# Two of the late modulation pairs are made in the second mixer's heads instead of the first FFN, with a smaller scratch for dynamic transfers

## The chip, the cores and the metric

The kernel runs on one core of one Trainium2 chip. The metric is device time in microseconds of one execution. Before the change the median of three runs is 1742.76 us (1740.17 to 1743.3).

## What is computed

Two layers of a diffusion backbone over 512 latent tokens and 256 context tokens of width 1024. Each layer has a mixer and a SwiGLU FFN (hidden width 2816), each between norms with a shift, scale and gate. The mixer of the first layer is gated linear attention beside grouped-query attention; that of the second is a bidirectional gated recurrence (HGRN2) with eight heads of 128. Only the latent tokens are returned.

The part that moves is the modulation. Each layer turns two vectors, one for latent tokens (`c`) and one for context tokens (`c_ctx`), into six vectors of 1024:

```python
sc = jax.nn.silu(c)
scc = jax.nn.silu(c_ctx)
for l in range(DEPTH):
    m_lat = jnp.split((sc @ mod_w[l] + mod_b[l])[:, None, :], 6, axis=-1)
    m_ctx = jnp.split((scc @ mod_w[l] + mod_b[l])[None, None, :], 6, axis=-1)
    h_lat = _modulate(_rms(x_lat, norm_pre_mix[l]), m_lat[0], m_lat[1])
    ...
    x_lat = x_lat + m_lat[2] * _rms(o_lat @ w_out, norm_post_mix[l])
    h_lat = _modulate(_rms(x_lat, norm_pre_ffn[l]), m_lat[3], m_lat[4])
    x_lat = x_lat + m_lat[5] * _rms(_swiglu(h_lat, ffn_w_gate[l], ffn_w_up[l], ffn_w_down[l]), norm_post_ffn[l])
```

In the last layer the context tokens end after the mixer's scan, so of its vectors 2, 3, 4 and 5 only the latent versions are needed. Vector 2 is first used behind the second mixer's heads, in its output projection; 3, 4 and 5 later still.

## The kernel before

Products of full precision are made of three products of rounded parts (`mm3`, L679): a weight is loaded raw, ScalarE rounds it to a high part and VectorE subtracts that for the low part (`unit`, L664 to L674). Such weight units go round in three raw buffers and four buffers of parts. SP issues all weight loads, in one queue.

The order: first mixer, output projection, first FFN (`ffn`, L1488), second mixer (`odd_mixer`, L1298), output projection, second FFN. A scheduler orders the instructions of each engine. Where `self.pinned` is set, TensorE's products stay in the order in which the program issues them; this holds for the heads of the second mixer and not for the FFN. The other engines' orders are the scheduler's in both.

**Modulation vectors** that are not needed at once are made on VectorE (`mod_vec`, L508 to L551), a generator that takes one small step whenever it is asked. For each job (two vectors) it loads `mod_w` in blocks of 128 x 1024 (512 KB, L454, two buffers `mraw`), one block ahead, and multiplies each block by a column of the activated vector into an accumulator (`macc`, L528 for the first block, L530 for the others). A job that makes latent and context versions of one vector has 8 blocks of two passes; a job with two vectors for the latent tokens alone has 16 blocks of one pass. Then TensorE sums the accumulators over the partitions (L537), VectorE copies the sum (`modrows`, L462), TensorE turns it (`modT`, L468) and VectorE adds the bias (L474). Where the vector is a gate, it is multiplied by a norm's gain (L576), turned (`gcT`, L580), copied (L582) and stored to DRAM (L584), from where it is later read as a row for all partitions. `modrows` and the gate's copy take turns in the same two `mraw` buffers.

**The first FFN** runs a loop over pairs of hidden blocks. A round has two products of gate and up weights by a seven-product scheme (`seven`, L768), whose weight sums VectorE makes (`pair_operands`, L730), and a product with the down weights for six token tiles, added to `y` on VectorE (L820). `fill` asks the modulation generator for a step at two places in `seven` and at the end of each token tile. All five jobs of `late_mods` (L1755) stand there.

**The second mixer.** First come value products (`odd_values`), then a loop over eight heads (L1415). A head has three weight units: two forget gates (`ff`, with a sigmoid on ScalarE at L1320) and the query (`fq`). Its recurrence (`scan`, L858) multiplies keys and queries by decays in seven doubling levels: at each level ScalarE copies half of the array (L923) and VectorE multiplies it (L928) and the decays (L929). TensorE makes small products from the levels (`pch`, `pbh`), turns the array (`knph`), makes the states' increments (`pdh`), and VectorE chains the states (L995); then TensorE makes the output (`poh`), and VectorE and GpSimd norm it (L1388, L598, L600, L1390). The loop interleaves three generators: `new` is the next head's products, `scan` and `outs` the recurrences of the heads before; `go` asks each of those named for one step.

Of the kernel before, what the change touches and what calls it, by code (L numbers as in the profile page):

```python
# [30 lines left out]
R_C, R_CC, R_NPM, R_MB, R_NQM, R_NPF, R_NQF, R_BG, R_LB, R_GG, R_HG, R_END = 0, 8, 16, 32, 128, 144, 160, 176, 180, 212, 213, 214  # L31
# [285 lines left out]
class Net:  # L317
# [980 lines left out]
    def odd_mixer(self, h, fi):  # L1298
        nc, I = self.nc, self.I
# [4 lines left out]
        with self.pool("hg") as gp:  # L1304
# [73 lines left out]
            def head(hd, arr, q, ks, f, S0):  # L1378
                def V(t, hh):
                    return fi[:, t, hd * P : (hd + 1) * P]  # L1380

                def evac(hh, t0, n, po):
                    o = fi[:, 0:LT, hd * P : (hd + 1) * P]
                    nc.scalar.copy(o, po)
                    sq = gp.tile([P, LT, P], F32, tag="sq", bufs=1, name="sq")
                    nc.scalar.activation(sq, po, AF.Square)
                    ss = self.sm.tile([P, LT], F32, tag="ss4", name="ss4")
                    nc.vector.tensor_reduce(ss, sq, axis=AX.X, op=ALU.add)  # L1388
                    rs = self.rstd(ss, P, LT)
                    nc.vector.tensor_tensor(o, o, rs[:, :, None].to_broadcast([P, LT, P]), op=ALU.mult)  # L1390

                return self.scan(gp, f"h{hd}", arr, q, ks, 1.0, f, LT, 1, V, S0, None, evac)

            def gate(c0):
                us = self.nat_units(w, 4 * D + c0, 256, 0) + self.nat_units(w, 4 * D + c0, 256, 1)

                def eo(t0, pt):
                    s = self.wp.tile([P, WU], F32, tag="mraw", bufs=2, name="silu")[:, :512].rearrange("p (a n) -> p a n", a=2)
                    nc.scalar.activation(s, pt[:, :, :256], AF.Silu)
                    o = fi[:, t0 : t0 + 2, c0 : c0 + 256]  # L1400
                    nc.vector.tensor_tensor(o, o, s, op=ALU.mult)

                for t0 in (0, 2):
                    self.gemm_nat(w, 4 * D + c0, 256, h, (t0,), eo, us=us)
                    yield
# [3 lines left out]
            def go(*xs):  # L1409
                for x in xs:  # L1410
                    next(x, None)

            self.pinned = True
            outs = old = scan = iter(())
            for hd in range(8):  # L1415
                given = []
                new = prep(hd, given)
                go(scan, new)
                go(outs, old)
                go(new, new)  # L1420
                go(outs, old, scan)
                go(new, new)
                go(scan, scan)
                outs, old, scan = scan, new, head(hd, *given[0])
            g = [gate(c0) for c0 in (0, 256, 512, 768)]
            go(scan, g[0])
            go(outs, old)
# [161 lines left out]
    def run(self):  # L1589
        nc, I, out = self.nc, self.I, self.out  # L1590
# [164 lines left out]
        def late_mods(pool):  # L1755
            return self.mod_vec(
                pool,
                (
                    (0, ((5, 0), (5, 1)), (5, R_NQF)),
                    (1, ((0, 0), (0, 1)), None),  # L1760
                    (1, ((1, 0), (1, 1)), None),
                    (1, ((2, 0), (3, 0)), (2, R_NQM, 1)),
                    (1, ((4, 0), (5, 0)), (5, R_NQF, 1)),
                ),
            )

        def ending(ys):
# [19 lines left out]
            return ender(ep, 0, 5, order, xat(x1), only_lat(xat(x2)), (1, 1, 0, R_NPM), h1), values(), ep  # L1787

        ys = self.ffn(0, ha, yp, fp, pp, rp, forms, ending, late_mods)
        fp.release()  # L1790

# [73 lines left out]
```

## Time and profile before

| What | Value |
|---|---|
| Median of three runs | 1742.76 us |
| Span of the profiled execution | 1746.0 us |
| The profiled execution's own time | not given apart from its span |
| Instructions | 33377 |
| DMA | 187.26 MB, mean 107 GB/s |
| ScalarE busy | 864.0 us (49%) |
| GpSimd busy | 73.5 us (4%) |

A profile is of one execution. Its lines give the source line, the engine (PE is TensorE, PEld its weight loads, DVE is VectorE, ACT is ScalarE, POOL is GpSimd, SP issues transfers), the operation, what is written from what, its shape, and how often. Matmuls are pipelined, so two of them overlap in the records and their spacing from start to start says what one costs. A wait is given as who waited for whom, with the total, the number of times and the longest.

### The profile page before, as it was taken

The page shows a single profiled execution, that of the slowest core. Times are in us where ns is not written, and L with a number is a line of the kernel's source. Part 1 is how long each engine was busy: PE and PEld are TensorE (multiplying, and loading weights), DVE is VectorE, ACT ScalarE, POOL GpSimd, SP SyncE. Part 2 cuts the span into 40 slices and gives each one's busy share as a digit, 9 for nine tenths or more (in the row PEclk, how much of TensorE's full clock was granted, in tenths as well). Part 3 has the DMA queues.
Part 4 walks back from the last instruction along what each step waited for, and adds up shares of the span by engine and source line. Part 5 has one row for each costly group of instructions (what it writes and reads, how often), then busy time and mean ns, then how long its engine had stood idle before and what let it go on. Part 6 is the DMA issues. An engine that isn't in the chain of part 4 may idle for free. (4 is left out here: it accounts for less than half of the span.)

```text
span 1746.0 us, 33377 instructions
## 1 busy us (share of the span) xinstructions
PE 1692.6 (97%) x13992; PEld 1536.0 (88%) x13992; DVE 1288.6 (74%) x2062; ACT 864.0 (49%) x1502; POOL 73.5 (4%) x93
## 2 busy tenths in 40 slices
PE   7999999999999999999999999999999999999998
PEld 5899987888999889898998998889898899999997
DVE  4889668736969999796668228887864678878785
ACT  4745567746442323333347336666643754344342
POOL 1004110000000000000001000000000000000000
PEclk9999999999999999999999999999999999999999
DMA  9641022144335465452234222111114333233333
GB/s 318 196 139 39 2 72 88 52 139 136 118 88 155 133 187 174 131 163 71 61 105 161 85 73 62 48 52 50 60 52 133 121 100 106 86 107 101 97 106 121
DMA packets 173937, 187.26 MB, mean 107 GB/s; under 512 B 6454, under 2 KB 149340, under 8 KB 173788
## 3 DMA queue, kind: packets, MB, share of 16 engines
q1 hardware_dynamic: 171856, 181.56, 33.6%
q10 hardware_dynamic: 1932, 3.59, 0.6%
q8 instruction: 109, 1.79, 0.4%
q14 instruction: 40, 0.33, 0.1%
HBM read 175.66 MB, written 9.46 MB: 106 GB/s over the span
## 5 line engine op out<-in xcount | busy, mean ns | idle before, releaser
L673 DVE TENSOR_TENSOR wL<-raw,wH 128x1024 fp32r<-128x1024 f32 (+1 forms) x126 | 151.0, 1205 | 114.7 <-ACT wH L672 114.5
L348 PE MATMUL nat<-wH,x 128*128 128x256 f32 (+1 forms) x1216 | 229.1, 287 | 3.0 <-ACT x L641 2.6
L727 ACT CAST wH<-raw 128x1024 fp32r<-128x1024 f32 x120 | 124.6, 1052 | 178.5 <-PE acc L348 70.8
L348 PEld LDWEIGHTS nat<-wH,x 128*128 128x128 f32 x1216 | 191.9, 191 | 8.0 <-ACT x L641 3.6
L728 DVE TENSOR_TENSOR wL<-raw,wH 128x1024 fp32r<-128x1024 f32 x120 | 145.1, 1219 | 64.0 <-ACT wH L727 64.0
L672 ACT CAST wH<-raw 128x1024 fp32r<-128x1024 f32 (+1 forms) x126 | 129.0, 1039 | 104.0 <-PE nat L348 31.4
L348 PE MATMUL acc<-wH,gH 128*128 128x512 f32 x440 | 172.6, 393 | 0.0
L348 PE MATMUL nat<-wL,x 128*128 128x256 f32 (+1 forms) x608 | 172.6, 284 | 0.0
L348 PE MATMUL acc<-wH,gL 128*128 128x512 f32 x440 | 171.7, 390 | 0.0
L348 PE MATMUL acc<-wL,gH 128*128 128x512 f32 x440 | 171.6, 390 | 0.0
L820 DVE TENSOR_TENSOR y<-y,acc 128x1024 f32<-128x1024 f32 x135 | 114.7, 861 | 31.6 <-PE acc L348 28.3
L348 PE MATMUL ff<-x,wH 128*128 128x512 f32 (+1 forms) x512 | 127.6, 340 | 0.0
L530 DVE SCALAR_TENSOR_TENSOR macc<-mraw,scT,macc 128x1024 f32<-128x1024 f32 x98 | 122.7, 1276 | 5.7 <-DMA mraw<-in_mod_w_dram 5.3
L600 POOL TENSOR_TENSOR rs<-ms,neghalf 128x1 f32<-128x1 f32 (+2 forms) x62 | 57.5, 928 | 1598.0 <-DVE ms L598 1597.9
L348 PEld LDWEIGHTS nat<-wL,x 128*128 128x128 f32 x608 | 116.5, 192 | 0.0
L348 PE MATMUL oproj<-wH,x 128*128 128x512 f32 x320 | 102.9, 398 | 3.6 <-ACT x L1235 3.6
L348 PEld LDWEIGHTS acc<-wH,gH 128*128 128x128 f32 x440 | 82.6, 188 | 19.8 <-issue 1.7
L348 PEld LDWEIGHTS acc<-wH,gL 128*128 128x128 f32 x440 | 82.6, 188 | 17.4
L348 PEld LDWEIGHTS acc<-wL,gH 128*128 128x128 f32 x440 | 82.7, 188 | 16.0
L348 PEld LDWEIGHTS ff<-x,wH 128*128 128x128 f32 x512 | 87.2, 190 | 10.1 <-issue 0.2
L923 ACT COPY qkh<-arr 128x512 f32<-128x512 f32 x112 | 70.1, 642 | 36.2 <-DVE arr L928 32.1
L348 PE MATMUL ff<-x,wL 128*128 128x256 f32 (+1 forms) x256 | 86.2, 337 | 0.0
(344 smaller groups left out, 4068.4 us busy)
## 6 DMA issues: line engine op xcount, KB each, us to landing
mraw<-in_mod_w_dram SPq DMA_DIRECT2D x80, 512.0 KB, 3.9
raw<-in_ffn_w_gate_dram SPq DMA_DIRECT2D x44, 512.0 KB, 3.8
raw<-in_ffn_w_up_dram SPq DMA_DIRECT2D x44, 512.0 KB, 4.5
raw<-in_ffn_w_down_dram SPq DMA_DIRECT2D x44, 512.0 KB, 3.6
raw<-in_odd_w_in_dram SPq DMA_DIRECT2D x40, 512.0 KB, 3.8
mraw<-in_mod_w_dram SPq DMA_DIRECT2D x32, 256.0 KB, 6.0
raw<-in_even_w_in_dram SPq DMA_DIRECT2D x16, 512.0 KB, 4.0
x<-xr SPq DMA_DIRECT2D x14, 512.0 KB, 2.7
```

Of the source, the lines that this page charges most:

```text
L348: return self.pin(self.nc.tensor.matmul(*a, **k))
L530: nc.vector.scalar_tensor_tensor(a, u, w, a, op0=ALU.mult, op1=ALU.add)
L600: nc.gpsimd.tensor_tensor(rs, ms, self.neghalf.to_broadcast([P, w]), op=ALU.pow)
L672: nc.scalar.copy(H[:, :m], raw[:, :m])
L673: nc.vector.tensor_tensor(L[:, :m], raw[:, :m], H[:, :m].bitcast(F32), op=ALU.subtract)
L727: self.nc.scalar.copy(H, f)
L728: self.nc.vector.tensor_tensor(L, f, H.bitcast(F32), op=ALU.subtract)
L820: nc.vector.tensor_tensor(y, y, pt, op=ALU.add)
L923: nc.scalar.copy(qkv[:, :, :, half, :], dst)
```

## The change

The last two jobs leave the FFN's list. The second mixer makes a generator of its own for them, with its accumulators in the heads' pool, and each of the six calls of `go` in a head's turn also asks it for a step; what is left after the eight heads is run out there. The program's scratch for dynamic transfers is set to 512 bytes per partition; before, it had its default size.

```diff
+            mods = self.mod_vec(gp, ((1, ((2, 0), (3, 0)), (2, R_NQM, 1)), (1, ((4, 0), (5, 0)), (5, R_NQF, 1))))
             self.pinned = True
             outs = old = scan = iter(())
             for hd in range(8):
                 given = []
                 new = prep(hd, given)
-                go(scan, new)
-                go(outs, old)
-                go(new, new)
-                go(outs, old, scan)
-                go(new, new)
-                go(scan, scan)
+                go(scan, new, mods)
+                go(outs, old, mods)
+                go(new, mods, new)
+                go(outs, old, scan, mods)
+                go(new, new, mods)
+                go(scan, scan, mods)
                 outs, old, scan = scan, new, head(hd, *given[0])
+            for _ in mods:
+                pass
...
                     (1, ((1, 0), (1, 1)), None),
-                    (1, ((2, 0), (3, 0)), (2, R_NQM, 1)),
-                    (1, ((4, 0), (5, 0)), (5, R_NQF, 1)),
...
-    nc = bacc.Bacc("TRN2", target_bir_lowering=False, num_devices=1)
+    nc = bacc.Bacc("TRN2", target_bir_lowering=False, num_devices=1, dynamic_dma_scratch_size=512)
```

Line numbers of the changed kernel are higher by one to three behind L1412.

## The prediction

> **What bounds the kernel now.** I read the page's first part, the stretches of time (windows) of the two stages that the change touches, then the timelines and waits inside them.
>
> ```profile
> PE 1692.6 (97%) x13992; PEld 1536.0 (88%) x13992; DVE 1288.6 (74%) x2062; ACT 864.0 (49%) x1502; POOL 73.5 (4%) x93
> ```
>
> TensorE is busy for 97% of a span of 1746.0 us, so almost any removed or added TensorE work counts in full, and VectorE's work counts only where TensorE must wait for it. The windows' columns are the stretch, its length, and busy time with counts of PE, PEld, DVE, ACT and POOL, then the granted clock.
>
> ```profile
> 616.10:807.50 191.40, 188.39 (x993) 170.98 (x992) 165.70 (x206) 65.51 (x91) 0.00 (x0) 1.00 0.51 156
> 840.16:886.54 46.38, 46.06 (x242) 42.56 (x242) 30.78 (x40) 16.15 (x22) 0.00 (x0) 1.00 0.23 68
> 977.00:1036.00 59.00, 59.00 (x470) 57.84 (x469) 8.74 (x9) 14.37 (x18) 0.00 (x0) 1.00 0.19 54
> 1089.86:1121.37 31.51, 31.51 (x400) 28.04 (x399) 25.12 (x56) 19.69 (x34) 1.44 (x1) 1.00 0.18 52
> ```
>
> The first row is four rounds of the first FFN's loop over hidden blocks, with the two moved pairs in them; VectorE is busy for 165.70 of 191.40 us and TensorE idles 3.0 us. The second is one round of the same loop after the modulation has ended: 46.38 us. The third lies between the FFN and the first head's recurrence: TensorE is full, VectorE has 50 us of nothing. The fourth is one steady head of the second mixer: 31.51 us, TensorE without a gap, VectorE at 25.12, so with 6.39 us to spare. In the whole stretch of the heads the list of waits has no row in which TensorE waits for VectorE or ScalarE; VectorE's own largest are these (total, times, longest):
>
> ```profile
> DVE wL L673 <- ACT wH L672: 30.6, 19, 6.4
> DVE ss L1388 <- ACT sq L1386: 20.5, 7, 3.3
> DVE y L1390 <- POOL rs L600: 6.6, 7, 1.2
> ```
>
> **The change part by part.** Moved are 32 loads of 512 KB, 32 VectorE passes, and per pair a TensorE sum over partitions, four transposes, one small transpose and six small VectorE operations.
>
> ```profile
> L530 DVE SCALAR_TENSOR_TENSOR macc<-mraw,scT,macc x98: 1266/1276/1285, 59.2 to 772.2; 128x1024 f32<-128x1024 f32 x98
> L528 DVE TENSOR_SCALAR macc<-mraw,scT x14: 741/746/754, 56.7 to 723.6; 128x1024 f32<-128x1024 f32 x14
> DMA to landing us min/median/max: 3.6/4.4/7.1
> ```
> ```profile
> 771.03 2.48 DVE L530 SCALAR_TENSOR_TENSOR macc<-mraw,scT,macc 128x1024 f32<-128x1024 f32 x2
> ...
> 802.54 0.69 DVE L462 COPY modrows<-mod_acc 128x512 f32<-128x512 f32 x1 [2.69 <-PE mod_acc L348]
> ```
>
> Of the 32 passes, 4 start a sum (0.746 us) and 28 add to it (1.276): 38.7 us of VectorE. Neighbouring operations overlap by some 0.07 (two passes end 2.48 after the first one's start), so in a queue a pass costs 1.2 and an opening 0.7.
>
> *Out of the first FFN.* In the instruction order of the changed program, the rounds behind the third pair are, on VectorE, the mod-free round of before with one weight split of another line in its place, so I price them at 46.38 us. Four rounds then take 185.5 instead of 191.4: 5.9 us less. But the third pair's closing also lies in that window and stays. What a closing costs TensorE:
>
> ```profile
> 712.60 0.39 PE L348 MATMUL acc<-wH,gL 128*128 128x512 f32 x1
> 712.92 1.06 PE L348 MATMUL mod_acc<-macc,one 128*32 128x512 f32 x8
> 713.91 0.50 PE L348 MATMUL acc<-wH,gH 128*128 128x512 f32 x1
> 714.25 0.39 PE L348 MATMUL acc<-wL,gH 128*128 128x512 f32 x1
> ...
> 716.77 0.60 PE L351 MATMUL modT<-ident,modrows 128*128 128x128 f32 x4
> 717.12 0.47 PE L348 MATMUL acc<-wH,gH 128*128 128x512 f32 x1
> 717.44 0.39 PE L348 MATMUL acc<-wL,gH 128*128 128x512 f32 x1
> ...
> 719.95 0.27 PE L351 MATMUL gcT<-ident,gc 128*8 128x128 f32 x1
> ```
>
> The neighbouring products follow one another at 0.23 us. From start to start the sum takes 0.99, the transposes 0.35, the gate's transpose 0.03, and the stream loses about 0.1 at each of three re-entries: 1.65 us. So the FFN gains 5.9 - 1.65 = 4.3 us; 3.3 of that is the two moved closings, 1.0 are waits of TensorE. Bounds: 1.8, if rounds are counted by VectorE's gating products (652.88 to 840.16 is 187.28 us against 185.5), and 5.9, if the third closing hides.
>
> ```profile
> 652.88:840.16 187.28, 185.53 (x976) 169.16 (x975) 152.07 (x194) 64.34 (x88) 0.00 (x0) 1.00 0.43 133
> ```
>
> *Into the heads, TensorE.* The two closings come back: +3.3 us, in a stage where TensorE has no gap. Both stand in the pinned order well behind their sums (the first in the third head's block, the second in the sixth's), so TensorE does not wait for the passes themselves. The closing's tiles take turns in the two banks that the head's transposes use; nearest rows give 0 to 1 us for that, and I take 0.
>
> *The first pair: into the trough.* In the changed order its 16 passes stand ahead of or among the weight splits of these rows, instead of in the heads proper:
>
> ```profile
> 977.17 0.06 DVE L1331 MEMSET pr<- 128x1 f32 x1
> 989.82 1.22 DVE L673 TENSOR_TENSOR wL<-raw,wH 128x1024 fp32r<-128x1024 f32 x1 [12.59 <-ACT wH L672]
> ...
> 1007.10 1.22 DVE L673 TENSOR_TENSOR wL<-raw,wH 128x1024 fp32r<-128x1024 f32 x1 [14.13 <-ACT wH L672]
> ...
> 1024.38 1.23 DVE L673 TENSOR_TENSOR wL<-raw,wH 128x1024 fp32r<-128x1024 f32 x1 [14.13 <-ACT wH L672]
> ```
>
> Two buffers, 4.4 us to land and 1.28 to use give two passes per 5.7 us. The first two are loaded by 977; the other 14 take 7 x 5.7 = 40 us and end near 1019, ahead of 1024. On the way a weight split comes 2 to 3 us late (the seventeen-microsecond rhythm is TensorE's, which frees the four weight buffers), and the unit in front of it, 24 products of 512 columns and 24 of 256 at 0.23 and half of that, keeps TensorE busy for 8 us. Cost 0. SP issues the loads in order with the weights' loads, so a weight load stands behind a modulation load that waits for its buffer; there are three raw buffers ahead of it, and I price that at 0 too. If this cover went, a late product would cost its lateness less those 8 us.
>
> *The second pair: into the fourth and fifth heads.* Here the order puts its 16 passes between the third head's and the fifth's operations: 2 x 0.7 + 14 x 1.2, with the 0.69 copy and five small operations 19.4 us. The three heads involved leave 3 x 6.39 = 19.2 us free, and not all of that can be filled: VectorE runs in order, and what waits for GpSimd's root (up to 1.2 each) or for a load holds everything behind it. So VectorE falls behind. How much TensorE allows is read from one head:
>
> ```profile
> 1097.86 1.29 DVE L928 TENSOR_TENSOR arr<-arr,f 128x512 f32<-128x512 f32 x2
> ...
> 1115.25 0.34 DVE L995 SCALAR_TENSOR_TENSOR Sh<-Sh,f,pdh 128x128 f32<-128x128 f32 x1
> ```
> ```profile
> 1104.98 0.88 PE L351 MATMUL knph<-ident,arr 128*128 128x128 f32 x6
> 1105.61 0.48 PE L348 MATMUL ff<-x,wH 128*128 128x256 f32 x2
> ...
> 1119.58 0.39 PE L348 MATMUL poh<-S,arr 128*128 128x128 f32 x2
> ```
> ```profile
> 1099.06 0.80 ACT L1320 ACTIVATE sg<-ff 128x768 f32<-128x768 f32 x1
> ```
>
> The array is ready at 1099.15 and turned by TensorE at 1104.98: 5.8 us. ScalarE, whose copies wait for VectorE's products, frees a bank at 1099.86 that TensorE needs at 1105.61: 5.7. The last state is ready at 1115.59 and used at 1119.58: 4.0. I then laid the changed order by hand on the two heads, each 31.5 us on. First head, up to the last product on the array: 1.7 us of closing operations and the first opening, 6.7 of passes and 0.8 of two operations put ahead, less 3.8 of idle time that they fill (3.3 of it the wait for the sum of squares): 5.4 us late. One load adds to it: its buffer is free at 1122.7 on the shifted scale, it is wanted at 1125.3 and there at 1126.3 to 1127.1 by 3.6 to 4.4 us of landing: 1.0 to 1.8, in the middle 1.4. To the second head it carries 5.4 + 2.4 (two passes) - 2.4 (two weight splits put off) - 1.2 (idle time) = 4.2; there come 6.0 of passes and 1.2 of a split, less 3.8: 7.6, with the load's 1.4 then 9.0. The array's 5.8 us of slack leave 3.2 for TensorE; the states of the first head, 4.2 + 1.4 - 4.0 = 1.6, are earlier and part of the same lateness. So TensorE loses **3.2 us**. Behind it VectorE has no passes left and wins back 6.4 us per head. Bounds: 0, if the slack takes it, and 9.0, if there is none to use.
>
> *The scratch.* The page's queues are all of hardware kind:
>
> ```profile
> q1 hardware_dynamic: 171856, 181.56, 33.6%
> q10 hardware_dynamic: 1932, 3.59, 0.6%
> ```
>
> No queue here takes its descriptors from an engine's program, and GpSimd issues no transfer. The space goes to the heads' pool (8 KB more per partition). Cost 0. The Trainium skill's "SBUF — State Buffer" (section "SBUF size: 192, 224, or 256?") calls this reserve the ring for software-made descriptors; no run here can show more than that no such queue appears.
>
> **Sum.** -4.3 + 3.3 + 0 + 3.2 = +2.2 us. The profiled span is 1746.0, which is 3.2 above the median of the runs shown (1742.76); I put the difference on the median: **1745.0 us**. Differences below 0.2% (3.5 us) are about what a measurement of this kernel can tell from none.
>
> **The rivals.**
>
> *VectorE sets the pace of two heads (slower).* Place: the passes between the recurrence's products in the fourth and fifth heads. For it: 19.4 us asked, 19.2 free; every load there must land within about 4.4 us or it holds the queue. Against it: 4 to 5.8 us of slack at each of three hand-overs. It decides from the point where VectorE is more than 9 us late at the end of a head. Price: the whole 9.0 instead of 3.2: -4.3 + 3.3 + 9.0 = +8.0, 1750.8 us.
>
> *The slack takes it all.* Landing nearer 3.6, and ScalarE's waits shrinking, keep the lateness under 5.8: -4.3 + 3.3 = -1.0, 1741.8 us. For it: TensorE shows no wait for either engine in the heads. Against it: the hand-laid 9 us.
>
> *The trough does not hold the first pair.* At 7.1 us of landing, the longest shown, 7 x 8.4 = 59 us end at 1036, 12 us behind the third split; less 8 us, +4 on the forecast: 1749.0.
>
> *The clock.* Rows of the timeline's windows with a reduced clock:
>
> ```profile
> 405.00:450.00 45.00, 42.56 (x230) 39.89 (x229) 37.50 (x43) 32.18 (x62) 2.57 (x4) 0.96 0.34 106
> 1305.00:1350.00 45.00, 41.39 (x261) 37.30 (x260) 18.76 (x23) 17.77 (x23) 1.01 (x1) 0.92 0.42 129
> ```
>
> Where TensorE idled 2.4 and 3.6 us, 4% and 8% of 45 us of clock went, 1.8 and 3.6 us. If shifted phases spare the one behind the heads and the slack holds, -1.0 - 3.6 = -4.6: 1738.2. If the waits in the heads add such a stretch, the forecast becomes +5.8: 1748.6. The Trainium skill's "TensorE: Matmul & The Clock Gate" (Part 1) says that one window of about 3.4 us without work halves the clock. My waits are pieces of one to two microseconds, so by that rule the heads keep their clock and the sum stays; the two rows agree with the rule as far as they go.
>
> *It does not do what it says.* The changed order shows no modulation pass behind the third pair in the FFN, and 32 in the second mixer; I leave this 2%.
>
> **How the numbers follow.** Forecast (0 to +5.5 us): 43%. VectorE sets the pace, with or without a clock stretch: 25%. Trough: 5%. Slack holds: 17%. Clock spared: 8%. Nothing moved: 2%. Beyond +3.5 lie the slower rivals and a third of the forecast, 44%; below -3.5 the spared clock and a little of the holding slack, 10%; between, 46%. The likeliest case's own range is 1742.5 to 1748.5. With 1739.0 to 1752.5 about one in ten stays out on each side; the ends are the spared clock nearly in full, and +8.0 with half of the FFN's low bound (2.5 us less gained) in.
>
> **What would show it.** Right: four rounds of the FFN at 46.4 us each; 16 passes between 977 and 1036 with VectorE idle under 30 us and TensorE unchanged; rows of waits of TensorE for VectorE or ScalarE in the fourth and fifth heads, 3 to 4 us in all; the other heads at 31.5. Wrong: no such rows (slack), 8 or more (pace), weight splits of that stretch after 1032 with TensorE waiting for them (trough), a window of the heads with a clock under 1.00, or FFN rounds away from 46.4.

## The result, and the profile after

The changed kernel takes 1745.72 us, the median of 20 runs (1743.38 to 1750.74), against 1742.2 us of 20 runs of the kernel before on the same chip: a ratio of 1.0022, 95% interval 1.0014 to 1.0029. On another chip it was 1748.25 against 1744.35 us, 1.0020 (1.0012 to 1.0029). Single executions of one kernel lie up to 7.4 us apart here, and the two profiled ones fell the other way round: the span is 1742.7 us after and 1746.0 before. So the two spans say nothing of the change; stages are compared.

The first part of the page after is that of before within 0.2%, GpSimd aside (72.7 against 73.5 us):

```profile
PE 1691.9 (97%) x13992; PEld 1535.6 (88%) x13992; DVE 1290.0 (74%) x2062; ACT 863.5 (50%) x1502; POOL 72.7 (4%) x93
```

No work went; it was moved. The stages show where. Of before, four rounds of the first FFN, from the start of the fifth round's gate products to that of the ninth's (columns as in the prediction: stretch, length, busy time of PE, PEld, DVE, ACT and POOL with counts, clock, DMA):

```profile
632.92:823.68 190.76, 187.75 (x988) 171.26 (x986) 159.73 (x202) 64.31 (x89) 0.00 (x0) 1.00 0.48 148
```

Of after, the same four rounds, the trough, and the steps from the second to the sixth turning of the array (`knph`):

```profile
632.01:816.20 184.19, 183.87 (x962) 170.20 (x960) 124.27 (x158) 64.65 (x89) 0.00 (x0) 1.00 0.23 69
966.00:1024.00 58.00, 57.98 (x462) 56.77 (x461) 27.66 (x25) 13.29 (x20) 0.00 (x0) 1.00 0.62 192
1096.66:1131.61 34.95, 33.66 (x415) 28.75 (x411) 30.76 (x66) 19.32 (x34) 1.01 (x1) 1.00 0.47 152
1131.61:1164.51 32.90, 31.74 (x402) 28.16 (x399) 31.89 (x63) 18.60 (x33) 1.01 (x1) 1.00 0.50 159
1164.51:1197.92 33.41, 31.76 (x402) 28.16 (x398) 29.71 (x63) 20.06 (x36) 1.43 (x1) 1.00 0.23 67
1197.92:1232.35 34.43, 33.45 (x416) 28.74 (x412) 26.38 (x63) 19.62 (x34) 1.36 (x1) 1.00 0.15 47
```

The FFN's four rounds are 6.6 us shorter in this pair of profiles. In the trough VectorE has 19 us more to do and TensorE is full, as before. Each of these four steps took 31.5 us before. Two have a closing (34.95 and 34.43), two between them have only passes (32.90 and 33.41); the first, sixth and seventh are unchanged. In that stretch TensorE now waits (total, times, longest):

```profile
PE pdh L348 <- DVE CTh L908: 2.8, 2, 1.7
PE modT L351 <- ACT kcn L1360: 1.0, 1, 1.0
PE kcT L351 <- DVE modcol L474: 1.0, 1, 1.0
PE mod_acc L348 <- ACT knh L975: 0.3, 1, 0.3
```

The last three stand round the closings, the first in the two steps between. From the first to the eighth `knph` the heads take 231.1 us instead of 221.7. Behind them, up to the output projection, it is 31.3 instead of 32.4: TensorE's wait there for ScalarE's copy of the turned output shrank from 3.6 to 2.5.

### The profile page after: what moved, and what is told of

Read it like the earlier page. It is cut to its first block, busy times and chain, and to the rows that moved or that the text cites. A ratio compares the mean times of both kernels' runs of the same rounds, so it can differ in the third digit from the quotient of the medians.

```text
span 1742.7 us, 33375 instructions
## 1 busy us (share of the span) xinstructions
PE 1691.9 (97%) x13992; PEld 1535.6 (88%) x13992; DVE 1290.0 (74%) x2062; ACT 863.5 (50%) x1502; POOL 72.7 (4%) x93
## 3 DMA queue, kind: packets, MB, share of 16 engines
q1 hardware_dynamic: 171856, 181.56, 33.1%
q8 instruction: 109, 1.79, 0.4%
```

## The experiments

The table has every kernel: ratio to the kernel before on the same chip with its 95% interval, four rounds of the first FFN as above, the heads from the first to the eighth `knph`, and their seven steps. One profile each.

| Kernel | Ratio | Four rounds | Heads | Steps |
|---|---|---|---|---|
| before | 1 | 190.8 | 221.7 | 31.5 31.5 31.6 31.5 31.5 31.5 32.4 |
| before_again | one execution, 1742.53 us | 190.6 | 221.6 | 31.5 31.5 31.5 31.5 31.5 31.5 32.4 |
| scratch_only | 0.9997 (0.9988 to 1.0006) | 190.1 | 221.7 | 31.5 31.5 31.6 31.5 31.5 31.5 32.5 |
| first_pair | 1.0001 (0.9992 to 1.0010) | 187.8 | 224.8 | 31.5 34.7 31.5 31.5 31.5 31.5 32.5 |
| after | 1.0022 (1.0014 to 1.0029) | 184.2 | 231.1 | 31.5 35.0 32.9 33.4 34.4 31.5 32.4 |
| after_again | 1.0020 (1.0012 to 1.0029) | 184.9 | 231.6 | 31.5 35.0 33.3 33.4 34.5 31.5 32.4 |
| before_few | 0.9988 (0.9977 to 0.9998) | 188.2 | 222.0 | 31.5 31.5 31.5 31.5 31.5 31.5 32.9 |
| after_few | 1.0001 (0.9991 to 1.0010) | 185.8 | 229.7 | 31.5 36.6 31.5 31.5 34.5 31.5 32.5 |
| shifted | 0.9999 (0.9991 to 1.0008) | 184.9 | 226.2 | 32.9 32.6 31.5 32.1 33.1 31.6 32.4 |
| spread | 1.0001 (0.9991 to 1.0011) | 185.4 | 226.0 | 32.9 33.3 31.5 31.5 31.5 31.5 33.7 |
| no_early_loads | 0.9990 (0.9981 to 0.9998) | 185.1 | 225.3 | 32.9 31.7 31.5 32.1 31.9 31.5 33.8 |
| late_close | 0.9987 (0.9975 to 0.9999) | 185.0 | 224.6 | 32.9 31.7 31.5 32.0 31.9 31.5 33.0 |
| gate_early | one execution, 1742.56 us | 184.7 | 226.8 | 32.9 33.0 31.5 32.0 31.9 31.5 34.0 |
| gate_late | 0.9982 (0.9973 to 0.9992) | 184.4 | 224.4 | 32.9 31.7 31.5 31.5 31.5 31.5 33.7 |

**What part of the change does what.** Four kernels were run side by side: both again, before with only the small scratch, and before with only the first pair moved:

```diff
-            mods = self.mod_vec(gp, ((1, ((2, 0), (3, 0)), (2, R_NQM, 1)), (1, ((4, 0), (5, 0)), (5, R_NQF, 1))))
+            mods = self.mod_vec(gp, ((1, ((2, 0), (3, 0)), (2, R_NQM, 1)),))
...
+                    (1, ((4, 0), (5, 0)), (5, R_NQF, 1)),
```

> The kernel before, unchanged, for a second profile. Theory (the two profiles at hand differ outside the changed stages only by how fast weight loads land in that execution): the first FFN's loop, 458.4 us in the first profile of before, moves by up to 3 us together with the second FFN's loop (310.8), and the eight heads, from the first turned array to the last, stay at 221.7 us within 0.3. Rival (the change itself speeds up the second FFN's loop to the 308.4 us of the changed kernel's profile): the second FFN's loop is again above 310.

> The changed kernel, unchanged. Theory: heads again 231 us within 0.5 (34.9, 32.9, 33.4 and 34.4 us in the third to sixth of the eight steps), the first FFN's loop 5 to 8 us under that of before_again, ratio 1.002. Rival (the lateness of VectorE depends on how fast loads land): the 32.9 and 33.4 us of the fourth and fifth steps move by over 1 us.

> The kernel before with the small scratch alone. Theory (no transfer uses the scratch): ratio 1.000 within 0.001, all stages as in before_again. Rival (other addresses or the scratch itself cost time): some part of the change's 1.0022, 1.001 or more.

> The change with only the first of the two pairs moved; the second stays in the first FFN. Theory (passes in the trough are free, a closing costs the heads about 3.2 us and the FFN's share of a pair is 2.5 to 3 us): the heads take 221.7 + 3.3 = 225 us, the fourth and fifth steps are back at 31.5, the FFN's loop is 2 to 4 us shorter than before's: ratio 1.000 within 0.001. Rival (the passes cost time in the trough too, by delaying weights): the stretch from the last gate product of the FFN to the first head grows by 1 us or more.

The repeats show the same stages to within 0.8 us. The second FFN, which nothing changed, takes 359.5 and 358.2 us from its first product to its last down product in the two profiles of before, 356.8 and 359.8 in those of after: single profiles differ by up to 3 us there, and the change doesn't speed it up. The scratch does nothing that can be seen. The first pair alone shortens the four rounds by 2.7 (187.8 against a mean of 190.5) and lengthens the heads by 3.1, all of it in the one step that has its closing: no net change. So the first pair's passes are free in the trough, and its closing costs as much in the heads as the whole pair did in the FFN.

**Passes or closings.** The 28 adding passes of both pairs are left out, once in the FFN and once in the heads; loads, opening passes and closings stay.

```diff
-                    else:
+                    elif len({m for m, _ in ms}) == 1:
                         nc.vector.scalar_tensor_tensor(a, u, w, a, op0=ALU.mult, op1=ALU.add)
```

> The kernel before without 28 of the 32 adding passes of the two pairs that the change moves (its vectors 2 to 5 of the second layer then lack their sums over blocks 1 to 7); loads, first passes and closings stay in the first FFN. It splits the FFN's gain. Theory: of the 5.7 us by which the first FFN's loop gets shorter when both pairs leave, 3.3 are the closings on TensorE and 2.4 are waits for a VectorE that the passes keep late: the loop is 455 instead of 457.2, ratio 0.9987. Rival (loads and closings make the waits as well, by their transfers and their PSUM banks): the loop stays at 457, ratio 1.000. Other rival (VectorE is what paces these rounds): 451.5 or less, ratio 0.9967.

> The changed kernel without the same 28 passes (vectors 2 to 5 of the second layer lack their sums over blocks 1 to 7); loads, first passes and closings stay in the heads. Theory: the lateness is the passes' VectorE time, so the steps of the fourth and fifth heads go from 32.9 and 33.4 back to 31.5, the two with a closing stay at 34.9 and 34.4, the stretch is 228, and the time 3.3 us below the changed kernel's, ratio to before 1.0002. Rival (the loads beside the weights', or the small operations of the closing, make the delay): the two steps stay above 32.5, the stretch at 231, ratio 1.002.

In the FFN (the row is of before_few) the passes are worth 190.5 - 188.2 = 2.3 us, as expected; 188.2 - 184.9 (the mean of the nine kernels without the pairs there) = 3.3 us are left for closings and loads.

```profile
631.01:819.21 188.20, 187.66 (x988) 171.31 (x986) 128.25 (x174) 65.18 (x89) 0.00 (x0) 1.00 0.47 150
```

In the heads the two steps between the closings go back to 31.5, with the loads of the second pair still coming (143 GB/s in the first):

```profile
1136.40:1167.89 31.49, 31.49 (x402) 28.10 (x399) 25.14 (x57) 19.73 (x34) 1.43 (x1) 1.00 0.46 143
1167.89:1199.42 31.53, 31.53 (x403) 28.10 (x399) 25.14 (x57) 19.72 (x34) 1.43 (x1) 1.00 0.18 52
```

So their 3.3 us are the passes' work on VectorE. The stretch missed its 228 by 1.7, all in the step with the first closing, 36.6: a wait of 1.4 in it was new, and is taken up below.

**The closing's place, and the passes' number.** `shifted` gives the generator its steps by a table: the sum over partitions behind `poh`, the transposes between the second gate's products and the query's, the gate's transpose in the next head, between `kcT` and `poh`. `spread` also keeps the second pair's passes in program order against one VectorE operation of each head, three to a head, with its closing among the gate's products.

```diff
+            plan = (
+                (1, 1, 1, 1, 1, 1),
+                (1, 1, 1, 1, 1, 1),
+                (1, 1, 2, 2, 1, 0),
+                (0, 0, 1, 1, 0, 1),
+                (0, 1, 0, 1, 0, 1),
...
-                go(outs, old, scan, mods)
-                go(new, new, mods)
+                go(outs, old)
+                ask(n[3])
+                go(scan, new)
+                ask(n[4])
+                go(new)
...
+                    if l == 1 and m > 3:
+                        self.pin(p)
```

> The changed kernel with each closing of the moved pairs put elsewhere in the head: the sum over partitions behind the output product (poh), the transposes between the second gate's products and the query's, the gate's transpose one head later, between kcT and poh. So the closing's tiles never stand between knph and kcT, where they share two PSUM banks with them. The passes keep nearly their places. Theory (bank waits): of the 3.4 and 2.9 us by which a head with a closing is longer than 31.53, only the 1.65 us of products stay and 1.2 to 1.7 go; the heads' stretch (first to eighth knph) is 228.3 instead of 231.1 to 231.6, with the lateness of the fourth and fifth heads still in it (3.3), and the time 3 us below the changed kernel's, ratio to before 1.0003. Rival (the closing itself costs this, by its re-entries and by the copies that TensorE's next step waits for): the heads stay at 231, ratio 1.002.

> As the kernel with shifted closings, and the second pair's 16 passes held to three in each of the fourth to eighth heads, with one behind them, by keeping them in program order against one operation of every head; its closing falls into the gate's products behind the heads. Theory (lateness comes from eight passes in one head, where VectorE has 6.4 us free): 3 x 1.2 = 3.6 us of passes fit into each head, the steps of the fourth and fifth heads go back to 31.5, the heads' stretch is 221.7 + 1.65 = 223.4 (one closing), the other 1.65 lies behind it; with an FFN 5.7 us shorter than before the time is 2.4 us below the kernel before, 1739.8, ratio 0.9986. Rival (any pass among the recurrence's products delays them, however few): each of five heads loses 0.4 to 1.2 us, the stretch is 225.5 to 229, ratio 1.000 to 1.002.

`shifted` does it: the steps with a sum and its transposes are 32.9 and 33.1 instead of 35.0 and 34.4, 3.4 us less in the two, more than expected, and the ratio to before is 0.9999. Its waits between knph and kcT are gone. Not expected was that the steps with passes alone also lost less, 0.6 instead of 3.3, though the passes lie in nearly the same heads. `spread` brings those steps to 31.5 exactly, as its theory had it, but its stretch is 226.0 and not 223.4, and its time that of before. A part of that was my sum (the second closing's 1.3 fell inside the stretch, not behind it); 1.7 are one wait in the second step, of the kind that after_few showed and `shifted` has too (1.0).

**One wait that nothing in the profile explains.** It stands behind the 128 small products (`pch`) in the loop's fourth turn. The profile names "issue": no semaphore, no engine. In the records of transfers, instructions come in blocks of 16 KB, on a queue of their own:

```profile
q8 instruction: 109, 1.79, 0.4%
```

No view names the queue's engine. I take it for TensorE's: of all bytes of instructions 84% come there (1.79 of 2.12 MB with the other such queue), and TensorE with its weight loads has 84% of the instructions (27984 of 33377).

Two pairs of kernels ask for the cause. `no_early_loads` starts the second pair's loads half a head later (its passes are then 2, 4, 4, 3 and 3 in the fourth to eighth heads) and turns the first pair's gate later too; `late_close` also puts the second closing behind the last gate products. `gate_early` and `gate_late` then exchange one thing between `no_early_loads` and `spread`, the place of the first gate's transpose:

```diff
+                if hd == 3:
+                    hold.pop()()
```

(behind the first gate's products in `gate_early`, between the second gate's and the query's products in `gate_late`).

> As the kernel with the passes spread, but with no load of the second pair before the second half of the fourth head; its passes are then 2, 4, 4, 3 and 3 in the fourth to eighth heads, and the first pair's gate is turned half a head later. It asks about a stall of 1.0 to 1.7 us, once, in the shifted, the spread and the thinned kernel: TensorE waits for nothing that the profile shows, behind 128 small products (pch) of the fourth head, with 250 to 310 GB/s of loads beside it, and goes on 1.4 us after a block of its instructions has landed in all three. Theory (the loads delay the instruction block): without loads there the stall goes, the heads' stretch is 224.3 instead of 226.0, ratio to before 0.999. Rival (the instructions inserted ahead of it shift where the blocks end, and the loads have nothing to do with it): the stall stays, 226, ratio 1.000. Four passes in a head (4.8 us) still fit: the fifth and sixth steps are 31.5; if not, they are 32 or more.

> As the kernel without early loads, and the second pair's closing put behind the last gate products, where TensorE waits 3.4 us for ScalarE's copy of the turned output (oproj <- ACT x). Theory: the sum over partitions and the transposes fall into that gap and cost TensorE nothing, the last step of the heads is 32.4 instead of 33.7 and the stretch from the last knph to the second output projection stays at 32.3; 1.3 us below the kernel without early loads, ratio to before 0.998. Rival (the copies of the closing on VectorE and the sum ahead of the turned output make that copy later): the stretch to the output projection grows by 1.0 to 2.0 and nothing is won.

> The kernel without early loads, but with the first pair's gate turned where the spread kernel turns it, between kcT and poh of the fourth head: the loads of the one, TensorE's order of the other up to the fourth head's small products. Theory A (the loads hold up the instruction block): no stall, the step from the second to the third knph is 31.6 to 31.7. Theory B (the inserted transpose shifts the instruction blocks against the small products): the stall of about 1.7 us is back without the loads, the step is 33.0 to 33.4.

> The spread kernel, with its three passes per head and its loads from the middle of the fourth head on, but with the first pair's gate turned as late as in the kernel without early loads, behind the query's products of that head. Theory A (loads): the stall of 1.7 us stays, second to third knph 33.2. Theory B (place of the instruction blocks): it goes, that step is 31.6, no pass delays a head (31.5 in the fourth to seventh steps), the heads' stretch is 224.3, and the time is that of before less 5.4 of the first FFN plus 2.7, ratio 0.9985.

Where the transpose stands decides whether the wait comes. gate_early, PE's timeline (start, length, operation, count, idle time before it):

```profile
1116.54 0.46 PE L348 MATMUL pch<-q,ks 128*32 128x32 f32 x32
1116.81 1.05 PE L348 MATMUL pch<-qkh 128*32 128x32 f32 x96
1119.25 0.61 PE L348 MATMUL ff<-x,wH 128*128 128x512 f32 x2 [1.39 <-issue]
```

gate_late, the same place:

```profile
1118.38 0.46 PE L348 MATMUL pch<-q,ks 128*32 128x32 f32 x32
1118.66 1.05 PE L348 MATMUL pch<-qkh 128*32 128x32 f32 x96
1119.64 0.73 PE L348 MATMUL ff<-x,wH 128*128 128x512 f32 x2
```

Counted from the first small product, the block of instructions sets out at +0.5 us in gate_early, and at -0.1, -0.1 and +0.8 in spread, shifted and after_few, which all stall; TensorE goes on 1.2 to 1.5 us after it has landed in all four. In gate_late, no_early_loads, late_close and after it sets out at -1.0, -1.1, -0.9 and -1.3, and nothing stalls. That fits theory B, that a single transposition ahead shifts where the block ends. But the time of the block alone doesn't make the wait: in the third turn of gate_late one sets out at +0.2, and for the last head of before one at +0.4, from the first of as many small products, and nothing stalls.

Nor is theory A, the loads, out. Moving the transpose moved a load as well, because the gate's copy takes its turn in the same two `mraw` buffers: the first load of the moved jobs near this place is issued at 1112.66 in gate_early, 3.9 us ahead of the small products, and at 1125.15 in no_early_loads, 9.4 us behind them. So gate_early is not the kernel without early loads that its expectation took it for. The last 3 us before the first small product (columns as above), gate_early and gate_late:

```profile
1113.54:1116.54 3.00, 3.00 (x29) 2.88 (x27) 0.49 (x3) 0.79 (x2) 0.00 (x0) 1.00 0.98 321
1115.38:1118.38 3.00, 3.00 (x28) 2.88 (x26) 1.22 (x4) 0.78 (x2) 0.00 (x0) 1.00 0.76 211
```

In these 3 us the four kernels that stall move 268 to 338 GB/s, and the ten others 169 to 211. So in these two pairs the place of the transpose decides (1.3 us for the step between gate_early and gate_late, one profile each); whether it does so by the block, by the load or by both is open. The kernel after, with its early transpose, doesn't stall; it moves 207 GB/s there.

`gate_late` is the version without any of the losses found. In its seven steps the list of waits of TensorE is empty, with three passes in each of the turns from the fourth on:

```profile
1068.11:1101.01 32.90, 32.90 (x415) 28.79 (x411) 25.81 (x61) 19.77 (x34) 1.02 (x1) 1.00 0.23 65
1101.01:1132.69 31.68, 31.68 (x403) 28.11 (x399) 26.42 (x60) 19.67 (x34) 1.44 (x1) 1.00 0.26 79
1132.69:1164.22 31.53, 31.53 (x402) 28.10 (x398) 28.36 (x60) 19.56 (x34) 1.43 (x1) 1.00 0.36 107
...
1258.83:1292.56 33.73, 33.73 (x486) 32.73 (x483) 27.85 (x60) 19.64 (x33) 1.01 (x1) 1.00 0.17 50
```

Its stretch is 224.4, expected 224.3; its ratio to before is 0.9982 (0.9973 to 0.9992), and so it is a little faster than both kernels. Here a closing costs 32.90 - 31.53 + 31.68 - 31.53 = 1.5 us, and the other 33.73 - 32.43 = 1.3.

`late_close` won nothing more. Its last step is 0.7 shorter than that of no_early_loads, and the way to the output projection 1.4 longer, because TensorE's order now has the closing ahead of the turned output, and the closing waits for VectorE:

```profile
1321.23 1.06 PE L348 MATMUL mod_acc<-macc,one 128*32 128x512 f32 x8
1323.55 0.63 PE L351 MATMUL modT<-ident,modrows 128*128 128x128 f32 x4 [1.26 <-DVE modrows L462]
1325.04 0.27 PE L351 MATMUL gcT<-ident,gc 128*8 128x128 f32 x1 [0.86 <-DVE gc L578]
1325.15 1.19 PE L351 MATMUL catT<-ident,y 128*128 128x128 f32 x8
```

## Why the forecast came out, and where its steps were off

The time, 1745.7 us, was within 1 us of the forecast, and its case (VectorE behind in two heads, TensorE losing about 3 us) is what happened. Part of the closeness is luck: the change was forecast at +2.2 us and measured at +3.8, against a kernel before whose median came out 0.6 lower than the one forecast from. The terms were less good than their sum; the first FFN's larger gain hides a part of what the closings cost too much:

| Term | Forecast | In the traces |
|---|---|---|
| First FFN | -4.3 | -5.6 |
| Two closings in the heads | +3.3 | +6.3 |
| First pair in the trough | 0 | 0 |
| Second pair among the recurrences | +3.2 | +3.3 |
| Scratch | 0 | 0 |
| Behind the heads | not named | -1.1 |
| Sum | +2.2 | +2.9 |

The ratio says +3.8 us (2.4 to 5.1); single profiles vary by up to 3 us in a stage that nothing changed, so the rest isn't assigned.

**The first FFN.** Four free rounds at 46.4 us were right: 185.5 forecast, 184.9 measured. The step that failed is "the third pair's closing also lies in that window and stays", with its 1.65 us. Counted from start to start of the rounds, four of them took 190.76 us with the two moved closings in them. My window of 191.40 ended at 807.50, ahead of the second moved closing's transposes (809.44), so what it had of the third pair's closing and what it lacked of the last one nearly balanced. It was only 0.64 us longer, and 1.65 was too much to take off. The split was off as well: "1.0 are waits of TensorE" is 2.3 by before_few.

**The closings.** The step that failed is "the closing's tiles take turns in the two banks that the head's transposes use; nearest rows give 0 to 1 us for that, and I take 0". One closing of after, PE's timeline without the gate products between:

```profile
1096.66 0.87 PE L351 MATMUL knph<-ident,arr 128*128 128x128 f32 x6
1097.80 1.06 PE L348 MATMUL mod_acc<-macc,one 128*32 128x512 f32 x8 [0.26 <-ACT knh L975]
...
1101.77 0.60 PE L351 MATMUL modT<-ident,modrows 128*128 128x128 f32 x4
1102.20 1.50 PE L348 MATMUL pdh<-y,knh 128*128 128x128 f32 x12
1103.54 0.38 PE L351 MATMUL kcT<-ident,kc 128*128 128x128 f32 x2
1104.90 0.41 PE L351 MATMUL kcT<-ident,kc 128*128 128x128 f32 x2 [0.97 <-DVE modcol L474]
```

The sum takes the bank of the first `knph`, the transposes that of the second, and so the second `kcT` needs a bank that VectorE's two additions of the bias (`modcol`) have not yet freed: 0.97 us. In the fifth step the transposes in their turn wait 1.0 for ScalarE's copy of `kcT`. Together 3.4 and 2.9 us instead of 1.65 each. That it is the place, and not the closing, is shown by shifted and gate_late, where one costs 1.3 to 1.5.

**The trough.** Right. The 16 passes are done at 1014.3, the row of the trough has TensorE at 57.98 of 58.00 us (VectorE idles 30.3, at the edge of the "under 30" that was to show it), and first_pair loses nothing but its closing. The rival of the trough is out.

**The second pair.** The size was right (3.2 forecast; 1.4 and 1.9 by the steps) and the place wrong. The step that failed is the list of three hand-overs, array, bank and state, with 4 to 5.8 us of slack each. None of them shows a wait. The one that does is a fourth: the states' increments (`pdh`) need the bank of the small products, which VectorE frees by a masked copy (`CTh`). In before:

```profile
1104.98 0.88 PE L351 MATMUL knph<-ident,arr 128*128 128x128 f32 x6
1107.31 0.29 DVE L908 COPY_PREDICATED CTh<-masks,pch 128x128 f32<-128x128 uint8 x1
1108.56 1.50 PE L348 MATMUL pdh<-y,knh 128*128 128x128 f32 x12
```

The copy ends at 1107.60, `pdh` begins at 1108.56: 0.96 us of slack. In after, VectorE's timeline behind the third `knph`:

```profile
1131.66 2.50 DVE L530 SCALAR_TENSOR_TENSOR macc<-mraw,scT,macc 128x1024 f32<-128x1024 f32 x2
...
1134.06 0.69 DVE L1348 TENSOR_TENSOR q<-q,fq 128x512 f32<-128x512 f32 x1
...
1136.06 0.31 DVE L908 COPY_PREDICATED CTh<-masks,pch 128x128 f32<-128x128 uint8 x1
```

and PE's:

```profile
1131.61 0.87 PE L351 MATMUL knph<-ident,arr 128*128 128x128 f32 x6
1136.52 1.58 PE L348 MATMUL pdh<-y,knh 128*128 128x128 f32 x12 [1.16 <-DVE CTh L908]
```

Counted from `knph`, the copy begins 4.45 us on instead of 2.33, which is 2.1 late; less 0.96 that is the 1.16 of the wait. Two passes, 2.50 us together, stand ahead of it in VectorE's order. The 9.0 us of lateness that I had summed up were not needed for this, and the rival "VectorE sets the pace", with its 9.0, is out: two passes, 2.5 us together, at the wrong place did it. That the 3.2 us worked out from the array's slack met the 3.3 of another hand-over is luck. after_few shows that the passes are the cause, and spread that three of them in a head cost nothing at their places. In those kernels number and place change together; a hint for the place is that the heads of no_early_loads with a fourth pass, which stands ahead of that copy, lost 0.5 and 0.4 us (the list of waits shows 0.2 of it) and those with three nothing. The other two rivals fall with this: the slack did not hold, and what was moved did leave the FFN.

**The clock.** No window of the heads has a clock under 1.00, in any kernel, though TensorE waited up to 1.7 us at a time. So the clock's two rivals are out: no stretch of half clock was added in the heads, and the one behind them came before and after alike (6.8 and 3.4 us long in these two profiles, 3.4 in before_again). The Trainium skill's rule on a window of 3.4 us without work ("TensorE: Matmul & The Clock Gate", Part 1) holds for the waits in the heads, and is too mild for the one behind them, as the last section shows. The two rows of the forecast did not both agree with that rule: in the first TensorE idled 2.44 us in one piece, and 1.8 us of clock went.

**Behind the heads.** I had left out that later heads give the next stage's weights time to come: the wait for the turned output fell by 1.1 us.

## What to carry to other kernels

Before work is put into a stage where another engine has time to spare, list every hand-over from that engine to the full one, PSUM banks that it frees by a copy included; the smallest slack (here 0.96 us) sets what may stand ahead of that hand-over, not the free time of the stage (6.4 us per head). A small sequence that shares banks with its surroundings costs by where it stands: the same closing took 3.4 us between two users of its banks and 1.5 with its steps apart. Move work in pieces that the slack takes, hold them there in the order, and read the steps of the loop one by one: the version made so is 0.18% faster than the kernel before, where the first form was 0.22% slower.

## What the runs showed of the hardware

Instructions arrive in 16 KB blocks over DMA while the program runs (109 blocks on the queue that I take for TensorE's). Behind 128 small products within 2 us TensorE stood still for 1.0 to 1.7 us in one turn of four of the fourteen kernels, with no semaphore in the profile, and went on 1.2 to 1.5 us after a block had landed. The place of one transposition decided it (gate_early 33.0, gate_late 31.7 us for the same step); whether through the blocks or through a load that moved with it is open.

Half a clock came after less idle time than I had thought. Behind the heads TensorE has one wait for ScalarE's copy of the turned output; it was 2.5 to 4.2 us long in twelve of the profiles, whose records of the granted clock have 3.4 or 6.8 us of half clock beginning within 2 us of its end, and 2.3 in after_again, which has none. In late_close it is split in three pieces of at most 1.3, and there is none either. After and after_again, the wait there:

```profile
PE oproj L348 <- ACT x L1235: 2.5, 1, 2.5
```
```profile
PE oproj L348 <- ACT x L1235: 2.3, 1, 2.3
```

The length of the wait alone doesn't decide. Ahead of the first FFN TensorE waits once for VectorE's normed tokens (`xn`), and in no_early_loads 1.93 us of that were followed by 3.4 us of half clock. The row of the 20 us around it has no other idle time, and a mean clock of 0.91:

```profile
426.19 1.66 PE L351 MATMUL hT<-ident,xn 128*128 128x128 f32 x8 [1.93 <-DVE xn L619]
420.00:440.00 20.00, 18.07 (x99) 17.78 (x98) 18.38 (x22) 13.70 (x29) 0.92 (x1) 0.91 0.44 141
```

In after the same wait took 1.87 us and no half clock followed. The Trainium skill's page named above speaks of a window of about 3.4 us without work; here 1.93 was enough, and the measurement decides.

The size of the scratch for dynamic transfers changed nothing that can be measured (0.9997, 0.9988 to 1.0006).
